# W_out's weight sums by VectorE from blocks on chip, and another order of loads and evictions around the last head pair

## The chip, the cores and the metric

The kernel runs on one core of one Trainium2 chip. The metric is the device time of one execution in microseconds (us). The times of before are three runs: 539.84, 540.49 and 540.99 us, median 540.49. The trace comes from one further, profiled execution.

## The reference, cut to what matters

One layer of a bidirectional trunk on a sequence of 512 positions and a model width of 1024, in float32. The change touches the output projection `mix @ w_out` of the attention half, and what stands around it.

```python
h = rms_norm(x, attn_norm_g)
xr, gate, q, k, v = split(h @ w_in)
y_rnn  = (rg_lru_fwd(conv(xr)) + rg_lru_bwd(conv(xr))) * gelu(gate)
y_attn = dilated_attention(q, k, v, rel_bias)      # 8 heads of 64
mix = concat(rms_norm(y_rnn, norm_rnn_g), rms_norm(y_attn, norm_attn_g))   # 512 + 512 columns
x = x + mix @ w_out                                # w_out: 1024 x 1024
h = rms_norm(x, mlp_norm_g)
x = x + square(relu(h @ w_up)) @ w_down
return rms_norm(x, final_norm_g)
```

## The kernel before, in words

**Products of three.** TensorE (PE) multiplies in a reduced float32. Each operand is split into a rounded part "hi" and a remainder "lo", and a product is three matmuls: hi·hi, hi·lo and lo·hi (`mm3`, L323 to L325). "A product" below means these three matmuls on a 128x128 by 128x512 tile. A weight tile of 128x1024 (512 KB) is split by `conv_hi` (L252, a copy by ScalarE, ACT) and `conv_lo` (L279, a subtraction by VectorE, DVE). Weights come through a stream of three buffers named `wraw`. `emit_dma` (L235) loads the next of the list `plain` each time `conv_lo` has freed a buffer.

**Attention.** Heads are handled in pairs 0 to 3, a pair in four quarters u = 0 to 3. For a pair and a quarter, PE computes the scores (`att_s`, L829, tile `ps` in two PSUM banks "gs"). DVE adds the bias and takes the extreme value (`att_e`, L846, one instruction per head, reading a bias tile `tw`), POOL (GpSimd) zeroes the edge of the tile (L845), and ACT takes the exponential (L847). One step of the outer loop later PE transposes the quarter (`att_t`, L867, tile `pt`) and ACT copies it out (L869). `att_av` (L969, tile `pav`) multiplies by the values. DVE then multiplies by the reciprocal sums `zrow`, giving `yp` (L975). The path to `zrow` is: reciprocal and spread by DVE (`att_z`, L891 and L893), a transpose by PE (`att_zt`, L897, tile `prow`), a copy by ACT (L898), and four transfers from SP's queue (`att_zd`, L905). `att_q` squares `yp` on ACT (L623), `att_y` adds the square to a running sum on DVE (L629), and `att_a` scales `yp` on ACT into `at` (L986). When all four pairs are in, PE turns the sum (L441, tile `pcs`), DVE reduces it (L446, L425) and POOL raises it to the power -1/2 (L428, `rcol`). Every eviction of the attention half of W_out needs this `rcol`.

Bias tiles: for each head and each of two variants, `load_tw` (L494 to L499) issues one transfer of 128x384 and two of 128x160 from a table in HBM into one of four `tw` buffers of 128x1024.

**Fillers.** Between these steps the loop `for i in range(5): for u in range(4)` puts independent products from a list (`fill`): first the projections of q and k, then 32 products of the recurrent half of W_out (`wo_thunks`), called b0 to b31 here. b0 to b15 make the left column half for the four row tiles tt, b16 to b31 the right half. A table `FILL` says how many fillers stand at the four places of a quarter; without an entry it is one each. After the fourth product of a row tile, DVE adds the PSUM tile to the residual: `x <- pwo` (L1022). In before this addition follows directly behind its last product on DVE's queue. When b0 comes up, `load_x` is called; it starts the loads of the residual x (eight tiles of 256 KB, L1064) and of W_out's attention half, spread over the following quarters by the list `more`.

**W_out's attention half by seven products.** The 2x2 block product is made with seven block products instead of eight (Winograd's form). The weights are four blocks named 11, 12, 21, 22 (512 KB each). Needed are 11, 21, 22 and the sums s1 = 11+12, s2 = 11+12+22, s3 = 12+22, s4 = 11+12+22+21, up to signs. The order of use is `OSEQ` = 11, s2, s3, s4, 21, s1, 22, four products each (`wo_m`, evicted by `wo_x`, L1205). In before the sums are made by the transfers. For each sum a plain load puts the first block into a part of the tile `ws` (L1067, SP's queue), and every further block is a transfer with `accum_op=add` from POOL's queue (L1070). Blocks 11, 21 and 22 come once more through the `wraw` stream. The row sums on the activation side (`o_sum`, `o_hi`, `o_lo`, `o_hi2`, `o_lo2`) are made by DVE and ACT from `at`. For 21 and s1 the remainder is made by `remake` (L262, L264): two negative copies by ACT, and two accumulating transfers from POOL's queue.

**Behind it** stands the up projection. Its first tiles n0, n1, n2 come through `wraw`, and its first sums t1, t2, t3 are loaded into `tw` buffers by `load_t` (L1180) and completed by accumulating transfers from POOL's queue (L1182).

**What sets the order.** The instructions of PE, ACT, DVE and POOL stay in the order in which the program issues them; each engine works through its list in order. The order of SP's transfers is set by the compiler's scheduler. A transfer waits for its buffer, and in SP's list each waits for the one eight places ahead of it. `BES` holds what stands beside each of the 28 products of the seven.

## Time and profile of before

The profiled execution took 539.57 us on the device; its span from the first to the last instruction was 537.8 us.

| | before |
|---|---|
| runs (us) | 539.84, 540.49, 540.99 |
| profiled execution | 539.57 us, span 537.8 us |
| granted TensorE clock, mean | 0.997 |
| PE busy | 525.1 us, 98% |
| DVE busy | 429.9 us, 80% |
| ACT busy | 358.4 us, 67% |
| POOL busy | 77.0 us, 14% |
| moved by DMA | 112.29 MB |

In a timeline a line has the start, the duration, the engine, the line of the code, the operation, what it writes and reads, and a count. In brackets stands the engine's idle time before it and what ended it. PE is a pipeline: the next matmul starts 0.23 us after the one before although each is listed as 0.39 us, so lost time is read from the starts. In the view of waits each line has who waited for whom, the sum in us, how often, and the longest.

### The profile page before, as it was taken

The numbers are of one execution on the slowest core, as the hardware profiler recorded it, in microseconds if no ns is written. First come the engines' busy times: TensorE is split into PE (matmuls) and PEld (weight loads), VectorE is DVE, ScalarE is ACT, GpSimd is POOL, SyncE is SP. The second block draws the span as 40 slices with busy tenths as digits, with TensorE's granted clock in tenths as the row PEclk, the third lists the DMA queues.
The fourth block names the chain that finished last, engine by engine and source line by source line (L and its number), as shares of the span: only waits on it lengthen the run. The fifth ranks groups of instructions, "written<-read, shape, count | busy, mean of one in ns | idle before, by whom it ended". The sixth has DMA issues, their size and how long they took to land.

```text
span 537.8 us, 8418 instructions
## 1 busy us (share of the span) xinstructions
PE 525.1 (98%) x3035; PEld 451.7 (84%) x3035; DVE 429.9 (80%) x636; ACT 358.4 (67%) x578; POOL 77.0 (14%) x128
## 2 busy tenths in 40 slices
PE   9999999999989889999999999999999999999995
PEld 7757888887877668889999888888999999888884
DVE  6998888996843688889769987879756978886985
ACT  7578946888845556586566855565656686755665
POOL 0282000000102241001030223001001120131000
PEclk9999999999999999999999999999999999999998
DMA  7745386687699969966686799994987497799804
GB/s 280 234 135 139 88 234 179 159 255 192 147 304 299 296 112 235 345 209 168 185 163 165 201 247 275 278 369 116 289 236 202 126 207 188 179 290 261 206 1 157
DMA packets 44298, 112.29 MB, mean 209 GB/s; under 512 B 5332, under 2 KB 15700, under 8 KB 44256
## 3 DMA queue, kind: packets, MB, share of 16 engines
q1 hardware_dynamic: 35536, 81.71, 46.1%
q0 software_dynamic: 8544, 29.81, 29.6%
q8 instruction: 24, 0.39, 0.3%
q10 hardware_dynamic: 176, 0.23, 0.1%
q14 instruction: 18, 0.15, 0.1%
HBM read 100.16 MB, written 4.23 MB: 194 GB/s over the span
## 4 chain that ended last, share of the span: by engine, by line
PE 86%; DMA 7%; DVE 4%; issue 1%; ACT 0%; SPq 0%; POOL 0%; DVEq 0%; ACTq 0%; POOLq 0%
PE pu L324 10%; PE pu L325 10%; PE pu L323 10%; PE pd L324 9%; PE pd L323 9%; PE pd L325 9%; PE pqk L323 3%; PE pqk L325 3%; PE pqk L324 3%; DMA tw<-in_w_up_dram 2%; PE ps L829 2%; DMA zrow<-z 2%; PE pv L323 2%; PE pt L867 1%; PE pg L543 1%; PE pwo L323 1%
## 5 line engine op out<-in xcount | busy, mean ns | idle before, releaser
L279 DVE TENSOR_TENSOR wlo<-wraw,whi 128x1024 fp32r<-128x1024 f32 x72 | 87.8, 1220 | 21.1 <-ACT whi L252 20.7
L252 ACT ACTIVATE whi<-wraw 128x1024 fp32r<-128x1024 f32 x69 | 72.9, 1058 | 39.3 <-PE pd L325 18.4
L324 PE MATMUL pd<-wlo,ah 128*128 128x512 f32 (+1 forms) x195 | 75.2, 386 | 0.0
L323 PE MATMUL pd<-whi,ah 128*128 128x512 f32 (+1 forms) x195 | 75.2, 386 | 0.0
L325 PE MATMUL pd<-whi,al 128*128 128x512 f32 (+1 forms) x195 | 75.2, 386 | 0.0
L252 ACT ACTIVATE whi<-tw 128x1024 fp32r<-128x1024 f32 x36 | 38.0, 1059 | 38.1 <-PE pu L324 8.1
L325 PE MATMUL pu<-hh,wlo 128*128 128x256 f32 x224 | 63.4, 283 | 0.0
L324 PE MATMUL pu<-hl,whi 128*128 128x256 f32 x224 | 63.4, 283 | 0.0
L323 PE MATMUL pu<-hh,whi 128*128 128x256 f32 x224 | 63.4, 283 | 0.0
L323 PE MATMUL pu<-h2h,whi 128*128 128x256 f32 (+1 forms) x200 | 60.1, 300 | 0.0
L324 PE MATMUL pu<-h2l,whi 128*128 128x256 f32 (+1 forms) x200 | 60.0, 300 | 0.0
L325 PE MATMUL pu<-h2h,wlo 128*128 128x256 f32 (+1 forms) x200 | 60.0, 300 | 0.0
L279 DVE TENSOR_TENSOR wlo<-tw,whi 128x1024 fp32r<-128x1024 f32 x36 | 44.0, 1222 | 18.4 <-ACT whi L252 18.3
L323 PEld LDWEIGHTS pu<-hh,whi 128*128 128x128 f32 x224 | 43.0, 192 | 0.0
L324 PEld LDWEIGHTS pu<-hl,whi 128*128 128x128 f32 x224 | 43.0, 192 | 0.0
L325 PEld LDWEIGHTS pu<-hh,wlo 128*128 128x128 f32 x224 | 43.0, 192 | 0.0
L325 PEld LDWEIGHTS pd<-whi,al 128*128 128x128 f32 x195 | 36.6, 188 | 7.4
L323 PEld LDWEIGHTS pd<-whi,ah 128*128 128x128 f32 x195 | 36.6, 188 | 7.4
L252 ACT ACTIVATE whi<-ts 128x1024 fp32r<-128x1024 f32 x24 | 25.5, 1061 | 26.0 <-PE pd L325 18.4
L324 PEld LDWEIGHTS pd<-wlo,ah 128*128 128x128 f32 x195 | 36.6, 188 | 7.2
L323 PEld LDWEIGHTS pu<-h2h,whi 128*128 128x128 f32 x200 | 38.3, 191 | 1.3
L324 PEld LDWEIGHTS pu<-h2l,whi 128*128 128x128 f32 x200 | 38.3, 191 | 1.3
(281 smaller groups left out, 1262.3 us busy)
## 6 DMA issues: line engine op xcount, KB each, us to landing
wraw<-in_w_up_dram SPq DMA_DIRECT2D x25, 512.0 KB, 3.8
ts<-in_w_dn_dram POOLq DMA_DIRECT2D x24, 512.0 KB, 13.3
wraw<-in_w_dn_dram SPq DMA_DIRECT2D x24, 512.0 KB, 9.6
tw<-in_w_up_dram SPq DMA_DIRECT2D x15, 512.0 KB, 9.8
tw<-in_w_up_dram POOLq DMA_DIRECT2D x15, 512.0 KB, 8.4
wraw<-in_w_in_dram SPq DMA_DIRECT2D x13, 512.0 KB, 4.1
ts<-in_w_dn_dram SPq DMA_DIRECT2D x8, 512.0 KB, 8.9
tw<-in_w_dn_dram SPq DMA_DIRECT2D x8, 512.0 KB, 8.5
```

The lines of the kernel that those rows point to most:

```text
L252: act(hi, raws[i], AF.Copy)
L279: nc.vector.tensor_tensor(lo, r, f(splits[i][0]), op=OP.subtract)
L323: nc.tensor.matmul(o, lhsT=a[0], rhs=b[0], start=bool(first), stop=False, skip_group_check=on)
L324: nc.tensor.matmul(o, lhsT=a[0], rhs=b[1], start=False, stop=False, skip_group_check=on)
L325: nc.tensor.matmul(o, lhsT=a[1], rhs=b[0], start=False, stop=bool(last), skip_group_check=on)
L543: nc.tensor.matmul(pg[2 * d + j][halves[b ^ d]], lhsT=gwr[t][halves[b], c], rhs=xc[t][halves[b]], start=True, stop=True)
L829: nc.tensor.matmul(psq[p][e][:, :NK], lhsT=sp[p, 0, n, e][:, c0:c0 + P], rhs=k, start=i == 0, stop=i == 1)
L867: nc.tensor.transpose(pt[:, i * P:(i + 1) * P], en[h][qt][:, k:k + P], ident)
```

## The change

Five things are changed:

1. `load_x`: only the blocks 12, 22 and 21 are loaded (SP's queue), and 11 comes through `wraw` as before. DVE makes the sums: `sum1` s1 = 12+11, `sum2` s2 = s1+22 (into a `tw` buffer), `sum3` s3 = 12+22 in place, and s4 = s2+21 (another `tw` buffer). All seven accumulating transfers of L1070 go, and so do the second loads of 21 and 22 through `wraw`.
2. `load_tw`: the two transfers of 128x160 become one with a pattern of 128x2x160.
3. `FILL`: three fillers instead of four in the first three quarters of step 3. The three products stand later instead, between the last `att_av` and the turn `pcs`, and behind that.
4. The addition `x <- pwo` of a row tile is put off to a later product (`end`), and the last one to behind the four products of block 11.
5. Around the last pair: `att_a` ahead of `att_q`; the row sums s1 and s2 of the second half, and the splits of the weights (`conv_hi`, `conv_lo`), stand at other products.

```diff
-    plain = deque(i for i, c in enumerate(chunks) if c is not None and not (isinstance(c, tuple) and c[1][0] in "st"))
+    plain = deque(i for i, c in enumerate(chunks) if c is not None and not (isinstance(c, tuple) and (c[1][0] in "st" or c[0] == "o" and c[1] != "11")))
...
-        for c, k in ((0, TH - WN - v), (WN + TH + P, P - 1 + v)):
-            nc.sync.dma_start(t[:, c:c + WN], bass.AP(tensor=nbd.tensor, offset=b + S + k, ap=[[1, P], [1, WN]]))
+        k = TH - WN - v
+        nc.sync.dma_start(bass.AP(tensor=t.tensor, offset=t.offset, ap=[t.ap[0], [WN + TH + P, 2], [1, WN]]),
+                          bass.AP(tensor=nbd.tensor, offset=b + S + k, ap=[[1, P], [P - 1 + v - k, 2], [1, WN]]))
...
+            if p == 3:
+                att_a(p)
             if p != 2:
                 att_q(p)
+            if p < 2:
                 att_a(p)
...
+        def end(n, tt):
+            stt(x1[tt, n], pw[n, tt], rc[0][:, tt:tt + 1], x1[tt, n], op0=OP.mult, op1=OP.add)
...
-                if b in (1, 17, 21, 25):
-                    conv_hi(C_WO + {1: 3, 17: 4, 21: 5, 25: 6}[b])
-                if b in (3, 19, 23, 26):
-                    conv_lo(C_WO + {3: 3, 19: 4, 23: 5, 26: 6}[b])
-                if k == 3:
-                    stt(x1[tt, n], o, rc[0][:, tt:tt + 1], x1[tt, n], op0=OP.mult, op1=OP.add)
+                if b in (1, 15, 18, 28):
+                    conv_hi(C_WO + {1: 3, 15: 4, 18: 5, 28: 6}[b])
+                if b in (3, 17, 20):
+                    conv_lo(C_WO + {3: 3, 17: 4, 20: 5}[b])
+                if n == 0 and tt and k == 3:
+                    end(0, tt - 1)
+                if n and (tt, k) == (0, 1):
+                    end(0, 3)
+                if n and k == 3 and tt < 3:
+                    end(1, tt)
             return run
+        st["wo"] = lambda: end(1, 3)
...
-        def w_add(n, b):
-            return lambda: nc.gpsimd.dma_start(ts[n], oblock(b), accum_op=OP.add)
+        def sum1():
+            tt(s1, b12, raws[C_WA], op=OP.add)
+
+        def sum2():
+            t = work.tile([P, 1024], FT, name="tw", tag="tw", bufs=4)
+            tt(t, s1, b22, op=OP.add)
+            chunk("s2", t)
+            t4 = work.tile([P, 1024], FT, name="tw", tag="tw", bufs=4)
+            chunk("s4", t4)
+            more[1].append(lambda: tt(t4, t, b21, op=OP.add))
+
+        def sum3():
+            tt(b12, b12, b22, op=OP.add)
...
+        w_in(b12, "12")()
         x_in(0, 0)()
-        x_in(1, 0)()
-        more.append([x_in(2, 0), x_in(3, 0), w_in("s2", "11")])
-        more.append([w_add("s2", "12"), w_in("s3", "12")])
-        more.append([w_add("s2", "22"), w_in("s4", "11")])
-        more.append([w_add("s3", "22"), w_add("s4", "12"), w_in("s1", "11")])
-        more.append([w_add("s4", "22"), w_add("s1", "12")])
-        more.append([w_add("s4", "21"), x_in(0, 1), x_in(1, 1)])
+        more.append([x_in(1, 0), w_in(b22, "22")])
+        more.append([x_in(2, 0), x_in(3, 0)])
+        more.append([sum1, w_in(b21, "21")])
+        more.append([sum2, x_in(0, 1)])
+        more.append([sum3, x_in(1, 1)])
         more.append([x_in(2, 1), x_in(3, 1)])
...
-    FILL = {(4, 0): (0, 1, 0, 0), (4, 1): (0, 1, 0, 1), (4, 2): (0, 1, 0, 0), (4, 3): (0, 1, 0, 0)}
+    FILL = {(3, 0): (1, 1, 1, 0), (3, 1): (1, 1, 1, 0), (3, 2): (1, 1, 1, 0), (4, 0): (0, 1, 0, 0), (4, 1): (0, 1, 0, 1), (4, 2): (0, 1, 0, 0), (4, 3): (0, 1, 0, 0)}
...
     fill(1)
     att_av(3, range(4))
-    att_y(3)
-    o_lo2(0)
-    fill(3)
-    rc[1] = rstd_cols(row_sums(turned(ssy[1], "gs")), S)
-    remake(C_WA + OSEQ.index("21"))
+    fill(1)
     o_sum("s1", 1)
     o_sum("s2", 1)
     o_hi("s2", 1)
+    fill(1)
+    att_y(3)
+    o_lo("s2", 1)
+    fill(3)
+    rc[1] = rstd_cols(row_sums(turned(ssy[1], "gs")), S)
+    fill(1)
+    conv_lo(C_WA + 2)
+    remake(C_WA + OSEQ.index("21"))
     fill(len(fillers))
...
-    BES["11"].update({1: lambda: (o_lo("s2", 1), o_hi2(1))})
-    BES["11"].update({2: lambda: o_lo("s1", 0)})
-    BES["21"].update({2: lambda: o_lo("22", 0)})
-    BES["s2"].update({1: lambda: o_lo2(1), 2: lambda: o_hi("s1", 1)})
-    BES["s3"].update({1: lambda: (o_lo("s1", 1), o_sum("22", 1)), 2: lambda: o_hi("22", 1)})
-    BES["s4"].update({1: lambda: o_lo("22", 1)})
-    BES["11"].setdefault(1, lambda: None)
-    also = BES["11"][1]
-    BES["11"][1] = lambda: (also(), remake(C_WA + OSEQ.index("s1")))
+    BES["11"].update({1: lambda: (o_hi2(1), remake(C_WA + OSEQ.index("s1"))), 3: lambda: st["wo"]()})
+    BES["s2"].update({1: lambda: conv_lo(C_WA + 3), 2: lambda: o_hi("s1", 1), 3: lambda: (conv_lo(C_WA + 4), o_lo2(0))})
+    BES["s3"].update({1: lambda: o_lo2(1)})
+    BES["s4"].update({1: lambda: (o_lo("s1", 0), o_sum("22", 1)), 2: lambda: o_hi("22", 1)})
+    BES["21"].update({1: lambda: o_lo("s1", 1), 3: lambda: (conv_lo(C_WA + 7), o_lo("22", 0), o_lo("22", 1))})
```

On the engines' lists this reads as follows. DVE gets four additions of 128x1024 and the same number of everything else. POOL's list loses the seven transfers. SP's list loses two loads of W_out, one of the first `ws` loads, and one transfer in each pair of bias transfers. PE and ACT have the same instructions in another order.

More of the change, by code (lines that the diff above doesn't have):

```diff
@@ L266, in emit_plain @@
     def emit_plain(i):
-        if chunks[i][1][0] != "s":
+        if chunks[i] == ("o", "11"):
             emit_dma()
@@ L282, in conv_lo @@
             if isinstance(c, tuple) and c[0] == "o":
-                if c[1][0] != "s":
+                if c[1] == "11":
                     emit_dma()
@@ L1057, in load_x, with chunk @@
         ws = big.tile([P, 4, 1024], FT, name="ws", tag="bigB")
-        ts = {n: ws[:, i, :] for i, n in enumerate(("s2", "s3", "s4", "s1"))}
-        for n, t in ts.items():
+        b12, b22, b21, s1 = [ws[:, i, :] for i in range(4)]
+        tt = nc.vector.tensor_tensor
+        def chunk(n, t):
             raws[C_WA + OSEQ.index(n)] = t
@@ L1064, in x_in, with w_in @@
             return lambda: nc.sync.dma_start(x1[g, n], xn[2 * g + n])
-        def w_in(n, b):
-            return lambda: nc.sync.dma_start(ts[n], oblock(b))
-        def w_add(n, b):
-            return lambda: nc.gpsimd.dma_start(ts[n], oblock(b), accum_op=OP.add)
-        x_in(0, 0)()
-        x_in(1, 0)()
-        more.append([x_in(2, 0), x_in(3, 0), w_in("s2", "11")])
-        more.append([w_add("s2", "12"), w_in("s3", "12")])
-        more.append([w_add("s2", "22"), w_in("s4", "11")])
-        more.append([w_add("s3", "22"), w_add("s4", "12"), w_in("s1", "11")])
-        more.append([w_add("s4", "22"), w_add("s1", "12")])
-        more.append([w_add("s4", "21"), x_in(0, 1), x_in(1, 1)])
+        def w_in(t, b):
+            return lambda: nc.sync.dma_start(t, oblock(b))
+        def sum1():
[9 more added lines that the diff above has]
+            tt(b12, b12, b22, op=OP.add)
+        for n, t in (("s3", b12), ("22", b22), ("21", b21), ("s1", s1)):
+            chunk(n, t)
+        w_in(b12, "12")()
+        x_in(0, 0)()
+        more.append([x_in(1, 0), w_in(b22, "22")])
[3 more added lines that the diff above has]
+        more.append([sum3, x_in(1, 1)])
         more.append([x_in(2, 1), x_in(3, 1)])
```

## The prediction

> **What bounds the kernel now.** I read the page first, then PE's waits, then the timelines around them.
>
> ```profile
> span 537.8 us, 8418 instructions
> PE 525.1 (98%) x3035; PEld 451.7 (84%) x3035; DVE 429.9 (80%) x636; ACT 358.4 (67%) x578; POOL 77.0 (14%) x128
> ```
>
> PE is the bound, and 12.7 us of the span are not its own. The view of its waits, whole trace, says which of these can be had:
>
> ```profile
> PE pcs L441 <- DVE ysq L629: 2.0, 1, 2.0
> PE pt L867 <- POOL e L845: 2.0, 1, 2.0
> PE prow L897 <- DVE z L893: 1.4, 1, 1.4
> ```
>
> These are three single waits; the view's two others are shorter and stand at the start, and the rest is the first load and the tail. All three lie around the last head pair. PE's timeline there:
>
> ```profile
> 152.16 0.39 PE L325 MATMUL pwo<-whi,yl 128*128 128x512 f32 x1
> 153.98 0.30 PE L897 MATMUL prow<-ident,z 128*128 128x128 f32 x1 [1.44 <-DVE z L893]
> ...
> 154.82 0.35 PE L829 MATMUL ps<-kk,qh 128*128 128x416 f32 x1
> ...
> 159.21 0.35 PE L829 MATMUL ps<-kk,qh 128*128 128x416 f32 x1
> ...
> 177.93 0.40 PE L325 MATMUL pwo<-whi,yl 128*128 128x512 f32 x1
> 180.30 1.09 PE L867 MATMUL pt<-ident,e 128*128 128x128 f32 x8 [1.97 <-POOL e L845]
> ...
> 184.29 3.02 PE L969 MATMUL pav<-ett,vs 128*64 128x416 f32 x24
> ...
> 189.20 0.40 PE L325 MATMUL pwo<-whi,yl 128*128 128x512 f32 x1
> 191.62 0.66 PE L441 MATMUL pcs<-ident,ysq 128*128 128x128 f32 x4 [2.02 <-DVE ysq L629]
> ...
> 192.81 0.40 PE L323 MATMUL pwo<-whi,oh 128*128 128x512 f32 x1
> ...
> 195.33 0.39 PE L325 MATMUL pwo<-whi,ol 128*128 128x512 f32 x1
> ...
> 198.97 0.50 PE L323 MATMUL pwo<-whi,oh 128*128 128x512 f32 x1
> ```
>
> Undisturbed, twelve starts take 195.33 - 192.81 = 2.52 us, 0.229 a step and 0.69 a product. Start to start, less one step, the three gaps lose 1.59, 2.14 and 2.19 us. From 192.81 to 198.97 stand 24 steps, 5.50 us undisturbed and 6.16 in the trace: 0.66 lost at the heads of products s2 and s3. Together 6.58 us.
>
> Why each gap is there, by the timelines of DVE, POOL and SP's queue and by the chain of waits:
>
> ```profile
> 151.69 0.75 DVE L1022 SCALAR_TENSOR_TENSOR x<-pwo,rcol,x 128x512 f32<-128x512 f32 x1 [3.01 <-DMA x<-in_xn_dram]
> ...
> 153.61 0.23 DVE L893 COPY z<-rz 128x128 f32<-128x128 f32 x1
> ...
> 163.29 0.59 DVE L846 CUSTOM_DVE_ANT_0 e<-ps,tw 128x416 f32<-128x416 f32 x1 [2.91 <-DMA tw<-nbd]
> ```
> ```profile
> 178.31 1.76 POOL L1070 DMA_DIRECT2D ws<-in_w_out_dram  x2 [11.85 <-DMA ws<-in_w_out_dram]
> 179.40 0.96 POOL L845 MEMSET e<- 128x96 f32 x2
> ```
> ```profile
> 176.25 2.65 SPq L905 DMA_DIRECT2D zrow<-z  x4
> ```
> ```profile
> 178.36 10.94 DMA zrow<-z
> ```
>
> First gap: the first residual addition stands ahead of the scores' eviction and of z in DVE's list, and waits for its x. Second: the memsets for the last quarter stand in POOL's list behind two accumulating transfers, which wait 11.85 us for earlier ones. Third: the last zrow transfer is 10.94 us under way, so yp, its square and the turn come late. The last two are transfers in each other's way; the window view shows how full the DMA engines are:
>
> ```profile
> 150.00:158.00 8.00, 6.57 (x37) 5.43 (x36) 3.88 (x12) 4.38 (x12) 1.30 (x3) 1.00 1.04 395
> 158.00:162.00 4.00, 4.00 (x24) 3.48 (x24) 1.35 (x3) 1.81 (x5) 0.00 (x0) 1.00 1.03 232
> ```
>
> The last two columns are the DMA share and GB/s: full in both, but at 232 instead of 395 GB/s once accumulations and bias tiles run.
>
> **The change part by part.**
>
> *Traffic.* By the code, 14 transfers of 512 KB bring W_out's attention half (three through wraw, four plain, seven accumulating); four remain. 10 x 0.524 = 5.2 MB go, which at 232 to 395 GB/s is 13 to 23 us of the engines' time.
>
> *Second gap.* POOL's list then has only memsets here, none behind a transfer. The full 2.14 us are taken as gone; were a memset still late, 0 to 2.14 would stay.
>
> *First gap.* The addition now follows z in DVE's list. At three products a quarter PE still makes b6 to b8 before prow, reaching it at 152.39; z then has only the two evictions ahead. They need the second head's bias tile:
>
> ```profile
> 144.34 0.91 SPq L498 DMA_DIRECT2D tw<-nbd  x2
> 145.34 2.60 SPq L1064 DMA_DIRECT2D x<-in_xn_dram  x4
> ```
> ```profile
> tw<-nbd SPq DMA_DIRECT2D x14, 80.0 KB, 4.7
> ws<-in_w_out_dram SPq DMA_DIRECT2D x4, 512.0 KB, 6.7
> ```
> ```profile
> DMA to landing us min/median/max: 4.3/7.4/13.4
> ```
>
> (The issues by line have the median time to landing last; the third view is of the ws tile, its eleven transfers of both queues.) Issued by 145.25 with 4.7 us to landing it is there at 150.0; one transfer fewer only helps. Eviction 0.59 (the row at 163.29), reciprocal about 0.2 and z 0.23: z ends near 151.3, a microsecond ahead of PE. The 1.59 us go.
>
> *DVE's four additions.* No row has this instruction; the nearest is the subtraction of the same shape from two on-chip tiles:
>
> ```profile
> 197.05 1.21 DVE L279 TENSOR_TENSOR wlo<-ws,whi 128x1024 fp32r<-128x1024 f32 x1
> ```
>
> 1.21 each, 4.8 us in all. A quarter of step 3 then asks DVE for two evictions (1.2), one residual addition (0.75, row 151.69) and one sum (1.21): 3.2 us. PE's quarter shrinks from 159.21 - 154.82 = 4.39 to 3.70, one product less. So 0.5 us are free in each, and the sums hide behind PE. Uncovered they would cost 4.8; below nothing isn't possible, since DVE makes nothing less.
>
> *The bias tiles of the last two quarters.* They are queued behind 12, two x, 22, kk, n1 and two x: 2.9 MB, from 150.0 on at 395 GB/s until 157.3. Two tiles of 352 KB follow, 0.72 MB at 395 to 232 GB/s: the second lands between 159.1 and 160.4, its eviction (0.59) ends between 159.7 and 161.0. PE, without the first gap and three products shorter, comes to the fourth quarter's scores at 159.21 + 4.37 - 1.59 - 2.07 = 159.9 and needs the second bank 0.4 later. So 0 to 0.7 us are lost; I take 0.4. The bound above is the landing of before (row 163.29, eviction ended 163.88): 3.5.
>
> *Third gap.* The last pav starts at 184.29 less both gaps and three products, 178.5, and ends near 181.4 (3.02, less the pipeline's overlap). zrow is issued 3.7 us earlier than at 176.25, the last of the four near 174.8, so it has 6.6 us. Ahead of it in SP's list stand three loads of 512 KB (n2, and two for t1 and t2), issued once DVE frees a wraw buffer near 166: 1.6 MB, 4 us at 395 GB/s, gone by 171. Taken: in time. With the 10.94 us of before it would land at 185.7 and cost 3.3. Five products, 3.45 us, now stand between this pav and pcs, instead of three. The chain on DVE and ACT:
>
> ```profile
> 189.48 0.69 DVE L975 TENSOR_TENSOR yp<-pav,zrow 128x512 f32<-128x512 f32 x1 [1.95 <-DMA zrow<-z]
> 190.87 0.69 DVE L629 TENSOR_TENSOR ysq<-ysq 128x512 f32<-128x512 f32 x1 [0.69 <-ACT ysq L623]
> ...
> 193.53 0.42 DVE L946 TENSOR_TENSOR osum<-at 128x256 f32<-128x256 f32 x1
> ```
>
> Some 0.25 until yp, 0.69, on DVE then a residual addition 0.75, two row sums 0.42 each, and the sum of squares 0.69: 3.2 us. (On ACT, at and the square end earlier.) The margin is 0.2 us; I leave 0.1 standing. Without the two products moved here 1.2 would be lost.
>
> *The head of s2 and s3.* From pcs PE has its own 0.44 and six products (4.12): s2 at 4.56. DVE has the sum of squares until 0.2 before pcs, then a split of 0.42 and two residual additions of 0.75, until 1.7 after it, then
>
> ```profile
> 192.74 0.68 DVE L446 TENSOR_REDUCE cs<-pcs 128x4 f32<-128x512 f32 x1
> 193.45 0.17 DVE L425 TENSOR_SCALAR rv<-cs 128x4 f32<-128x4 f32 x1
> ```
> ```profile
> 193.71 1.14 POOL L428 TENSOR_TENSOR rcol<-rv,mhalf 128x4 f32<-128x4 f32 x1 [6.28 <-DVE rv L425]
> ```
>
> 0.68, 0.17, rcol 1.14, the first eviction 0.75, and 0.3 of hand-overs (an estimate: 0.1 each, as from 193.62 to 193.71): 4.7. 0.1 lost at s2. At s3 a conversion of 1.21 stands between two evictions as before: 0.25, and 0.1 at s4. I put 0.45 against the 0.66.
>
> A conversion now runs on DVE beside rcol. The start of the kernel shows the same pair:
>
> ```profile
> 22.48 1.34 POOL L428 TENSOR_TENSOR rcol<-rv,mhalf 128x4 f32<-128x4 f32 x1 [18.73 <-DVE rv L425]
> ...
> 22.96 1.23 DVE L279 TENSOR_TENSOR wlo<-wraw,whi 128x1024 fp32r<-128x1024 f32 x1
> ```
>
> rcol took 1.34 and ended (23.82) before the conversion did (24.19): 0 to 0.2 more than 1.14, 0.1 taken. [...]
>
> *Moved loads behind it.* Two tw buffers now hold s2 and s4, so the load for the second group's t1 waits until s4 is converted, near 193, instead of issuing at 167. It stalls nothing: PE waits for no load anywhere after 199, and SP's next load waits for a wraw buffer until about then in before too. Zero; with that cover gone, its landing time.
>
> *Sum.* Lost now 6.58; left 0.4 + 0.1 + 0.45 + 0.1 = 1.05. Gain 5.5. The profiled execution, 539.57 on the device around its span of 537.8, would be 534.0; the median of runs is 540.49, 0.9 above it, so 534.9. Bounds: all of it gone, 540.5 - 6.6 = 533.9, less 0.6 of spread between runs; the bias tiles or zrow as late as before, 538.2.
>
> **The rivals.**
>
> 1. *Bias tiles as late as before.* 3.1 us more than taken: 538.0. For it: they share a queue with as many bytes as before. Against: the accumulation at 155 is gone.
> 2. *zrow as slow as before.* It lands at 185.7: 3.3 us, 538.2. For it: three loads stand right ahead of it, as four did. Against: they are issued 6 us earlier, and no accumulation runs beside; up to 6.6 us under way costs nothing.
> 3. *Slower: DVE's list waits for block 12.* sum1 stands ahead of the evictions of the second quarter. Issued near 145.3, with the plain 6.7 us, block 12 is there at 152.0, when DVE comes to it. Each microsecond beyond 153 holds up scores and transposes one for one. With the 13.4 us of the longest ws transfer it lands at 158.7: 5.7 us, all of the gain. The bias tiles of the third quarter, eight places behind in SP's list, are then issued so late that about 1 us more is lost: 541.6. It decides from 158.5 on. Against: that longest transfer ran beside accumulations.
> 4. *rcol waits until the conversion beside it has ended.* For it: both read on-chip tiles, and the conversion starts first. Against: the rows at 22.48 and 22.96. Price 1.1 us (1.21 less the 0.1 taken): 536.0.
> 5. *The change does not do what it says.* The three waits are replaced by others of the same size, since DVE and SP serve the same deadlines: 540.5.
>
> **How the numbers follow.** Forecast 0.68, its own range 533.3 to 536.2; rival 1 0.09, rival 2 0.07, rival 3 0.08, rival 4 0.03, rival 5 0.05. About 0.2% (1.1 us) is what a measurement tells from no change. Faster: forecast and rivals 1, 2, 4, 0.87; same: rival 5, 0.05; slower: rival 3, 0.08. The range goes from 533.3 to 538.2, with rivals 3 and 5 outside.
>
> **What would show it.** PE's waits must lose pt behind POOL and prow behind z, and pcs behind ysq must fall below 0.3. DMA must move about 107 MB instead of 112.29. Bias tiles: the wait of the eviction e for tw in the last two quarters, below 1.5 us without a wait of ps. The sums: DVE must wait for no ws transfer. rcol under 1.4 us. Wrong would be a new wait of PE's ps or pt for DVE above 1 us.

## The result, and the profile after

The changed kernel takes 534.99 us, the median of four runs (533.74, 534.94, 535.03 and 536.40), beside 540.24 us for the kernel before on the same chip. The ratio is 0.9902 with a 95% interval of 0.9875 to 0.9929, so about 5.3 us are gained. Measured twice more, on other occasions, the medians are 535.11 and 534.97 us, and the ratios 0.9898 [0.9880, 0.9916] and 0.9901 [0.9884, 0.9918].

The profiled execution of the changed kernel is its longest run, 536.40 us. That matters below: some of what its trace shows is larger there than in two further traces of the same program. First its page:

```profile
span 534.6 us, 8387 instructions
...
DMA packets 42602, 107.05 MB, mean 200 GB/s; under 512 B 4916, under 2 KB 15284, under 8 KB 42560
```

5.24 MB less are moved than before, ten blocks of 0.524 MB as counted. PE's waits in the same trace:

```profile
PE ps L830 <- DVE mn L847: 1.3, 1, 1.3
...
PE pwo L323 <- DVE x L1231: 0.2, 1, 0.2
```

The three waits of before (pcs, pt, prow) are gone from the list. Two new ones of this stretch stand there: the scores `ps`, and the head of product s2. The line numbers have moved: L830 was L829, L847 was L846, the evictions `wo_x` are L1231, the residual additions L1014. PE's timeline at the places of the three old gaps and of the two new ones:

```profile
144.09 0.40 PE L323 MATMUL pwo<-whi,yh 128*128 128x512 f32 x1
...
153.33 0.39 PE L325 MATMUL pwo<-whi,yl 128*128 128x512 f32 x1
153.56 0.27 PE L898 MATMUL prow<-ident,z 128*128 128x128 f32 x1
...
161.36 0.35 PE L830 MATMUL ps<-kk,ql 128*128 128x416 f32 x1
163.06 0.45 PE L830 MATMUL ps<-kk,qh 128*128 128x416 f32 x1 [1.35 <-DVE mn L847]
...
178.62 0.39 PE L325 MATMUL pwo<-whi,yl 128*128 128x512 f32 x1
178.85 1.04 PE L868 MATMUL pt<-ident,e 128*128 128x128 f32 x8
...
187.48 0.39 PE L325 MATMUL pwo<-whi,yl 128*128 128x512 f32 x1
187.71 0.60 PE L441 MATMUL pcs<-ident,ysq 128*128 128x128 f32 x4
...
192.03 0.39 PE L325 MATMUL pwo<-whi,ol 128*128 128x512 f32 x1
192.66 0.50 PE L323 MATMUL pwo<-whi,oh 128*128 128x512 f32 x1 [0.25 <-DVE x L1231]
...
198.45 0.39 PE L323 MATMUL pwo<-whi,oh 128*128 128x512 f32 x1
```

prow, the last pt and pcs each start one step (0.23 us) behind the matmul ahead of them: all three gaps are zero. At 163.06 the second bank of the last quarter's scores is 1.70 us behind the matmul before it, one step of which is 0.19: 1.51 us lost. s2 (192.66) loses 0.40. The first row is b0, the last the head of product s4; these two instants bound the stretch that the change touches. DVE in that stretch:

```profile
154.70 1.22 DVE L1084 TENSOR_TENSOR ws<-ws,wraw 128x1024 f32<-128x1024 f32 x1
...
157.51 1.22 DVE L1088 TENSOR_TENSOR tw<-ws 128x1024 f32<-128x1024 f32 x1
160.41 0.59 DVE L847 CUSTOM_DVE_ANT_0 e<-ps,tw 128x416 f32<-128x416 f32 x1 [1.68 <-DMA tw<-nbd]
...
162.41 0.59 DVE L847 CUSTOM_DVE_ANT_0 e<-ps,tw 128x416 f32<-128x416 f32 x1 [1.40 <-DMA tw<-nbd]
...
189.59 0.17 DVE L425 TENSOR_SCALAR rv<-cs 128x4 f32<-128x4 f32 x1
189.67 1.22 DVE L279 TENSOR_TENSOR wlo<-ws,whi 128x1024 fp32r<-128x1024 f32 x1
191.78 0.17 DVE L1265 TENSOR_SCALAR nrc<-rcol 128x4 f32<-128x4 f32 x1 [0.90 <-POOL rcol L428]
```

The first two sums (154.70, 157.51) take 1.22 us and start without an idle time: no wait for a block. The other two (162.92, 169.16) do the same. The evictions of the last quarter wait 1.68 and 1.40 us for their bias tiles. POOL's power, beside the conversion of 189.67:

```profile
189.84 1.91 POOL L428 TENSOR_TENSOR rcol<-rv,mhalf 128x4 f32<-128x4 f32 x1 [25.90 <-DVE rv L425]
```

It takes 1.91 us instead of 1.14 in before. The transfers of zrow, by the view of that tile's issues from 150 to 184 (the last line of the answer):

```profile
DMA to landing us min/median/max: 2.1/2.1/5.8
```

In before the same view says 4.9/10.8/12.1. The view holds two head pairs; the four transfers of the last pair land 2.1 us after their issue, and the 5.8 belongs to the pair before it. The next table gives starts of PE read from the timelines; "a0" and "a1" are the two further traces of the changed kernel.

| | before | after | a0 | a1 |
|---|---|---|---|---|
| profiled execution, us | 539.57 | 536.40 | 535.11 | 534.11 |
| start of b0 | 142.91 | 144.09 | 143.82 | 143.02 |
| start of s4 | 201.82 | 198.45 | 197.15 | 196.15 |
| b0 to s4 | 58.91 | 54.36 | 53.33 | 53.13 |
| s4 to the last matmul | 329.80 | 329.85 | 329.84 | 329.86 |

Behind s4 nothing changes. In the stretch from b0 to s4 the change gains 4.55, 5.58 and 5.78 us. Ahead of b0 the trace of after is 1.18 us later than before's. 0.54 of this are there at the very first scores (96.40 beside 95.86); a0 and a1 have them at 96.26 and 95.40, so this part varies from one execution to the next. 0.63 are lost between 110 and 117, which experiments 1 and 2 look into.

### The profile page after: what moved, and what is told of

The parts are those of the page before. It is cut to its first block, busy times and chain, and to the rows that moved or that the text cites. A ratio compares the mean times of both kernels' runs of the same rounds, so it can differ in the third digit from the quotient of the medians.

```text
span 534.6 us, 8387 instructions
## 1 busy us (share of the span) xinstructions
PE 525.5 (98%) x3035; PEld 451.3 (84%) x3035; DVE 434.6 (81%) x640; ACT 359.1 (67%) x578; POOL 72.3 (14%) x121
## 4 chain that ended last, share of the span: by engine, by line
PE 85%; issue 8%; DVE 3%; DMA 1%; POOL 1%; SPq 0%; ACT 0%; DVEq 0%; POOLq 0%; ACTq 0%
PE pu L324 10%; PE pu L323 10%; PE pu L325 10%; PE pd L323 9%; PE pd L324 9%; PE pd L325 9%; PE pqk L323 3%; PE pqk L325 3%; PE pqk L324 3%; PE ps L830 2%; PE pv L323 2%; PE pg L544 1%; PE pv L324 1%; PE pp L323 1%; PE pp L325 1%
## 5 line engine op out<-in xcount | busy, mean ns | idle before, releaser
L279 DVE TENSOR_TENSOR wlo<-wraw,whi 128x1024 fp32r<-128x1024 f32 x71 | 86.7, 1221 | 23.2 <-ACT whi L252 22.8
L252 ACT ACTIVATE whi<-wraw 128x1024 fp32r<-128x1024 f32 x67 | 70.8, 1059 | 37.0 <-PE pd L325 19.3
L252 ACT ACTIVATE whi<-tw 128x1024 fp32r<-128x1024 f32 x38 | 40.2, 1060 | 39.4 <-DMA tw<-in_w_up_dram 12.0
L279 DVE TENSOR_TENSOR wlo<-tw,whi 128x1024 fp32r<-128x1024 f32 x38 | 46.5, 1222 | 19.1 <-ACT whi L252 19.1
L325 PEld LDWEIGHTS pu<-h2h,wlo 128*128 128x128 f32 x200 | 38.3, 191 | 1.3
```

The lines of the kernel that those rows point to most:

```text
L252: act(hi, raws[i], AF.Copy)
L279: nc.vector.tensor_tensor(lo, r, f(splits[i][0]), op=OP.subtract)
L325: nc.tensor.matmul(o, lhsT=a[1], rhs=b[0], start=False, stop=bool(last), skip_group_check=on)
```

## The experiments

Twelve runs were made, of ten kernels. They ask what the small new losses are and whether they belong to the program (1 to 4), what each part of the change is worth alone (5, 6), what slack is left (7, 8), and whether a better version follows (9).

**1. The changed kernel again** (two runs of the same program, a0_after and a1_after).

> The changed kernel once more, to see which of its small losses come back. If they belong to the program: PE waits about 1.5 us for the second bank of the last quarter's scores (161.4 to 163.1), some 0.6 us are lost between 110 and 117 behind a late ql, rcol takes about 1.9 us and s2 starts 0.4 us late; the time is 534 to 536. If they are chance of one execution: at least two of the four are gone or below half.

> The changed kernel once more, beside e9_again on one chip: 534.5 to 535.5, with the same late s2 (0.40 us) and a wait for the second bank of the last quarter's scores between 0.4 and 1.5 us.

535.11 us (534.71 to 535.92) and 534.97 us (534.11 to 535.79). PE in a0 at 110, at the prow behind it and at the second bank, and then PE in a1 at 110:

```profile
110.54 0.35 PE L830 MATMUL ps<-kk,qh 128*128 128x416 f32 x1
110.73 0.35 PE L830 MATMUL ps<-kk,ql 128*128 128x416 f32 x1
...
114.17 0.30 PE L898 MATMUL prow<-ident,z 128*128 128x128 f32 x1 [0.16 <-DVE z L894]
...
161.00 0.35 PE L830 MATMUL ps<-kk,ql 128*128 128x416 f32 x1
161.77 0.46 PE L830 MATMUL ps<-kk,qh 128*128 128x416 f32 x1 [0.42 <-DVE mn L847]
```
```profile
109.68 0.35 PE L830 MATMUL ps<-kk,qh 128*128 128x416 f32 x1
110.01 0.46 PE L830 MATMUL ps<-kk,ql 128*128 128x416 f32 x1
```

0.77 - 0.19 = 0.58 us are lost at the second bank, and 0.39 in a1, against 1.51 in the first trace. The loss between 110 and 117 comes back in both, not always in the same place. a0 loses nothing at 110, but its prow at 114.17 is 0.31 late: the eviction ahead of z begins only after 1.31 us of idle time on DVE. a1 loses 0.14 at 110 (109.68 to 110.01, less 0.19), as after does, and more behind it. From the first scores to b0 PE takes 47.05 us in before, 47.69 in after, 47.57 in a0 and 47.62 in a1. rcol (1.91) and s2 (0.40 and 0.41) come out the same each time. So three of the four losses belong to the program, and the second bank's, below half in both, varies from one execution to the next.

**2. Bias tiles by three transfers again.**

```diff
-        k = TH - WN - v
-        nc.sync.dma_start(bass.AP(tensor=t.tensor, offset=t.offset, ap=[t.ap[0], [WN + TH + P, 2], [1, WN]]),
-                          bass.AP(tensor=nbd.tensor, offset=b + S + k, ap=[[1, P], [P - 1 + v - k, 2], [1, WN]]))
+        for c, k in ((0, TH - WN - v), (WN + TH + P, P - 1 + v)):
+            nc.sync.dma_start(t[:, c:c + WN], bass.AP(tensor=nbd.tensor, offset=b + S + k, ap=[[1, P], [1, WN]]))
```

> Each bias tile again by three transfers (one of 128x384, two of 128x160) instead of two. Theory (the merged transfer stands ahead of the second ql in SP's list and makes it land late): that ql lands 3 to 4 us after its issue instead of 5.9, and PE's delay of 0.6 us between 110 and 117 is gone. Rival (the ql is late for other reasons, such as the traffic of the moment): the delay stays. In the last two quarters 1 transfer more for each tile either costs nothing (the wait for the second bank stays 1.5 us) or makes it 0.3 to 1 us longer.

535.66 us, ratio 0.9904 [0.9883, 0.9924]. The view of the two ql transfers of pair 1 in SP's queue, first of a0 and then of this kernel:

```profile
DMA to landing us min/median/max: 3.2/4.4/5.7
```
```profile
DMA to landing us min/median/max: 3.2/3.2/3.2
```

The second ql stands behind the merged transfer in SP's list. In all seven traces with the merged transfer there it lands 5.7 to 6.1 us after its issue. In the seven traces with two separate ones, the kernel before among them, the view rests on one landing, that of the first ql (3.1 to 3.5 us); it has none for the second. The single packets in the traces settle it: the last packet of the second ql ends 2.4 to 2.6 us after the issue with separate transfers, and 4.8 to 5.2 us after it with the merged one. The late landing costs PE at the scores only where the issue is late as well: issued at 104.53 (a0) it is in time, at 105.15 (experiment 3's trace) PE waits 0.4 us for it and 0.55 are lost, and here an issue at 105.13 costs nothing.

The late ql is not the whole loss between 110 and 117. From the first scores to b0 this kernel takes 47.22 us, and the other six with separate transfers there take 47.04 to 47.37 and, in one case, 47.60: `best` (experiment 9), whose prow is 0.35 late behind a bias tile. Of the seven with the merged transfer six take 47.55 to 48.11, and experiment 4's takes 47.11. Nor is it shown that the merging does it. Merged, both strips of 128x160 stand ahead of the second ql; separate, one of them stands behind it. No run puts two separate strips ahead.

The other side: with one transfer more for each tile the second bank loses 1.05 us here, more than in a0 and a1 and less than in the first trace of after. So the theory holds for the ql, and the time shows no gain.

**3. Two residual loads behind the last bias tiles.**

```diff
-        more.append([x_in(2, 0), x_in(3, 0)])
-        more.append([sum1, w_in(b21, "21")])
-        more.append([sum2, x_in(0, 1)])
+        more.append([])
+        more.append([sum1, w_in(b21, "21"), x_in(2, 0)])
+        more.append([sum2, x_in(3, 0), x_in(0, 1)])
```

> The loads of x(2,0) and x(3,0) are put behind the last pair's second two bias tiles in SP's list. Theory (the bias tiles are late because SP issues them only once transfers eight places ahead have landed, and two x loads of 256 KB stand right ahead): the tiles are issued about 2 us earlier, PE's wait for the second bank of the last quarter falls from 1.5 us to below 0.3, and the time is 1 to 1.5 us shorter. Rival (the tiles share the DMA engines with whatever else is under way): the issues come earlier but the landing hardly does, and the wait stays above 1 us.

534.84 us, ratio 0.9888 [0.9869, 0.9908]: not to be told from the changed kernel. SP now issues the strips of the two tiles at 152.78 and 154.12 instead of 153.89 and 155.55 in a0. DVE's two evictions:

```profile
158.58 0.59 DVE L847 CUSTOM_DVE_ANT_0 e<-ps,tw 128x416 f32<-128x416 f32 x1 [0.34 <-PE ps L830]
...
161.22 0.59 DVE L847 CUSTOM_DVE_ANT_0 e<-ps,tw 128x416 f32<-128x416 f32 x1 [2.04 <-DMA tw<-nbd]
```

The first tile is now there before PE's scores are. The second, issued 1.4 us earlier, lands at 161.1, where it landed in a0 (161.0). Of the two readings each is right for one tile: the first was late by its issue, and the second was not. That what moves beside it holds it fits, but no run shows this alone. PE's loss at the second bank is 0.25 us, 0.14 to 0.33 less than in a1 and a0; a gain of 1 to 1.5 us is not there.

**4. No conversion beside rcol.**

```diff
     fill(1)
-    conv_lo(C_WA + 2)
     remake(C_WA + OSEQ.index("21"))
...
-    BES["11"].update({1: lambda: (o_hi2(1), ...
+    BES["11"].update({1: lambda: (conv_lo(C_WA + 2), o_hi2(1), ...
```

> The conversion of s3 is put behind the first eviction of product 11, so that no VectorE instruction with two on-chip inputs runs beside rcol. Theory (POOL's rcol is held while such an instruction runs): rcol takes 1.0 to 1.2 us instead of 1.91, nrc follows at once, and s2 starts without its wait of 0.4 us; a few tenths may come back at s2's second half, where the conversion now stands ahead of an eviction. Rival (rcol's length is something else, such as its place behind a long pause of POOL): it stays near 1.9 us.

534.61 us, ratio 0.9892 [0.9868, 0.9917]. POOL's timeline, and PE's at the head of s2:

```profile
188.14 1.01 POOL L428 TENSOR_TENSOR rcol<-rv,mhalf 128x4 f32<-128x4 f32 x1 [25.88 <-DVE rv L425]
```
```profile
190.32 0.39 PE L325 MATMUL pwo<-whi,ol 128*128 128x512 f32 x1
190.55 0.39 PE L323 MATMUL pwo<-whi,oh 128*128 128x512 f32 x1
```

rcol is back at 1.01 us, and s2 starts without a loss (0.23, one step). At s2's second half 0.08 and at s3's second half 0.22 us are lost instead (in a0 0 and 0.08), because the conversion now stands between the evictions of product 11 and delays those behind it. From the head of 11 to the head of s4 PE takes 8.76 us, against 8.93 in a0: 0.17 gained, as the trace shows it; too little for the medians.

**5. The kernel before, with the residual additions of the first column half put off, and nothing else.**

```diff
-                if k == 3:
-                    stt(x1[tt, n], o, rc[0][:, tt:tt + 1], x1[tt, n], op0=OP.mult, op1=OP.add)
+                if n == 0 and tt and k == 3:
+                    end(0, tt - 1)
+                if n and (tt, k) == (0, 1):
+                    end(0, 3)
+                if n and k == 3:
+                    end(1, tt)
```

> The kernel before, with one part of the change alone: each residual addition of the first half of the columns is put off by one product, so that the first no longer stands ahead of z in VectorE's list. Theory (the second gap is set by transfers that end at their own time, full DMA engines from 150 on, and the bias tiles are late too): the 1.59 us in front of prow go, but PE waits as much longer for ps or pt, and the time falls by 0 to 0.5 us, not 1.6. Rival (the transfers move forward with PE, or the gaps are independent): the time falls by 1.4 to 1.7 us.

540.69 us beside 540.86, ratio 1.0004 [0.9987, 1.0021]: nothing. PE's waits:

```profile
PE pt L867 <- POOL e L845: 2.4, 1, 2.4
PE pcs L441 <- DVE ysq L629: 1.9, 1, 1.9
PE ps L829 <- DVE mn L846: 1.8, 1, 1.8
```

The wait for prow is gone, and in its place PE waits 1.8 us for the scores (DVE sits idle 3.7 us for a bias tile) and 0.4 more for pt. The 1.59 us of the first gap were not to be had alone: the transfers came at their own time, and PE, earlier by that much, waited longer for them.

**6. The kernel before, with the sums on VectorE, and nothing else.** `load_x` is that of the change, with the three edits that go with it; the other parts of the change are left out.

```diff
-    plain = deque(i for i, c in enumerate(chunks) if c is not None and not (isinstance(c, tuple) and c[1][0] in "st"))
+    plain = deque(i for i, c in enumerate(chunks) if c is not None and not (isinstance(c, tuple) and (c[1][0] in "st" or c[0] == "o" and c[1] != "11")))
...
-        if chunks[i][1][0] != "s":
+        if chunks[i] == ("o", "11"):
...
-                if c[1][0] != "s":
+                if c[1] == "11":
```

> The kernel before, with the weight sums on VectorE and the loads that go with them, and nothing else: bias tiles by three transfers, the old places of the residual additions, four products in each quarter of step 3, the old order behind the last pav. Theory (the traffic makes most of the loss): POOL's memsets are no longer late and the 2.14 us before pt go, zrow lands within 6 us and the wait of pcs falls from 2.0 to below 1.3 us, the first gap stays at 0.8 to 1.6 us; together 3 to 4.3 us faster than before. Rival (the order of the lists makes most of it): less than 2 us faster, with new waits of PE for VectorE where the sums stand in its list.

538.42 us, ratio 0.9959 [0.9944, 0.9975]: about 2.2 us faster (0.9959 of 540.86), and not the 3 to 4.3 expected. The profiled execution is the longest of its ten runs, 540.62 us. PE:

```profile
154.03 0.39 PE L325 MATMUL pwo<-whi,yl 128*128 128x512 f32 x1
157.52 0.30 PE L897 MATMUL prow<-ident,z 128*128 128x128 f32 x1 [3.10 <-DVE z L893]
```

No wait for pt is left, the last pair's zrow lands 2.1 us after its issue, and pcs, 2.19 us late in before, is 0.17 late, with the old order behind the last pav. So the second and the third gap both went with this part alone, the accumulating transfers and the loads that they needed. The first gap has doubled, to 3.26 us: in the new `load_x` block 12 stands ahead of x(0,0), and the addition, still ahead of the evictions and of z, waits 4.68 us for its x. The window view of that stretch (its last three columns are the granted clock, the DMA share and GB/s) shows a second price:

```profile
154.00:157.50 3.50, 0.42 (x2) 0.01 (x1) 2.23 (x8) 0.98 (x3) 0.00 (x0) 1.00 1.05 406
157.50:159.00 1.50, 1.48 (x6) 1.30 (x7) 1.50 (x2) 0.66 (x3) 0.00 (x0) 0.73 1.03 391
159.00:161.00 2.00, 2.00 (x10) 1.84 (x9) 1.37 (x5) 0.04 (x1) 0.00 (x0) 0.50 1.20 327
161.00:163.00 2.00, 2.00 (x11) 1.74 (x10) 0.00 (x0) 1.67 (x5) 0.00 (x0) 0.85 0.63 188
```

After the 3.1 us without work the granted clock falls to 0.50. From prow to the second matmul behind pt PE takes 4.31 us (157.52 to 161.83); in experiment 5, at full clock, the same stretch takes 2.67 (152.62 to 155.29). So 1.6 us more are lost.

**7. Three products back in the quarters of step 3.**

```diff
-    FILL = {(3, 0): (1, 1, 1, 0), (3, 1): (1, 1, 1, 0), (3, 2): (1, 1, 1, 0), (4, 0): (0, 1, 0, 0), (4, 1): (0, 1, 0, 1), (4, 2): (0, 1, 0, 0), (4, 3): (0, 1, 0, 0)}
+    FILL = {(4, 0): (0, 1, 0, 0), (4, 1): (0, 1, 0, 1), (4, 2): (0, 1, 0, 0), (4, 3): (0, 1, 0, 0)}
```

> The changed kernel with four products instead of three in each of the first three quarters of step 3, so that three products fewer stand behind the last pair: one fewer between the last pav and pcs, two fewer between pcs and s2. Theory (those products cover the chain on VectorE and POOL): pcs waits 0.2 to 0.5 us, s2 starts 1.5 to 2.2 us late instead of 0.4, and the wait for the second bank, 0.6 us or more, goes since PE comes there later; 0.7 to 2 us slower than the changed kernel. Rival (the products are as good in the quarters): no difference above 0.5 us.

537.54 us, ratio 0.9945 [0.9924, 0.9967]: 2.6 us slower than a1 beside it. PE's waits:

```profile
PE pwo L323 <- DVE x L1231: 1.1, 1, 1.1
PE pcs L441 <- DVE ysq L630: 0.8, 1, 0.8
...
PE ps L830 <- DMA ql<-ql: 0.5, 1, 0.5
PE pt L868 <- ACT e L848: 0.5, 1, 0.5
```

With one product fewer ahead of it pcs loses 0.96 us, with two fewer ahead of it s2 loses 1.23 instead of 0.41, and one pt waits 0.46 for the exponential. The wait for the second bank is gone, as expected. From b0 to s4 PE takes 55.39 us, 2.26 more than in a1: 0.96 + 0.82 + 0.46 - 0.39, and 0.4 in small pieces. That is above the 2 us expected at most, since pcs lost twice what was expected and the wait of pt wasn't foreseen. (The late ql of this trace stands ahead of b0 and is not in the sum.) The moved products do cover the chain, and none is to spare.

**8. The first two sums made twice.**

```diff
-            tt(s1, b12, raws[C_WA], op=OP.add)
+            for _ in range(2):
+                tt(s1, b12, raws[C_WA], op=OP.add)
...
-            tt(t, s1, b22, op=OP.add)
+            for _ in range(2):
+                tt(t, s1, b22, op=OP.add)
```

> The changed kernel with the first two of the four sums made twice, 1.21 us more of VectorE's time in each of two quarters. Theory (about half a microsecond is free in the first quarter, where the sum stands ahead of both evictions, and over a microsecond in the second, where VectorE waits for a bias tile anyway): 0.4 to 1 us are lost at the transposes of the quarter behind the first sum, nothing at the second, and as PE comes later to the last quarter its wait for the second bank shrinks: 0 to 0.7 us slower. Rival 1 (there is no free time): 2 us or more slower. Rival 2 (VectorE isn't near the path): no loss in front of pt or ps beyond the wait for the bias tiles.

535.09 us, ratio 0.9900 [0.9877, 0.9923]: no slower. DVE:

```profile
154.27 2.48 DVE L1085 TENSOR_TENSOR ws<-ws,wraw 128x1024 f32<-128x1024 f32 x2
...
158.34 2.48 DVE L1090 TENSOR_TENSOR tw<-ws 128x1024 f32<-128x1024 f32 x2
160.73 0.58 DVE L847 CUSTOM_DVE_ANT_0 e<-ps,tw 128x416 f32<-128x416 f32 x1
```

Behind the first pair the four score matmuls of the next quarter start over 0.81 us (157.30 to 158.11) instead of 0.57, so 0.24 are lost there, at ps and not at pt as expected. Behind the second pair the eviction starts without a wait for its tile: the time was idle anyway, and the second bank loses 0.16. From b0 to s4 PE takes 53.40 us, beside 53.33 in a0 and 53.13 in a1. Rival 2 is the nearer one: even twice the work in these two quarters lies beside PE.

**9. Versions put together.** `best` has the edits of experiments 3 and 4, and of 2 for pairs 0 to 2 alone. `e7_stt` adds one: the residual addition of row tile 2 goes from ahead of cs to behind rv, beside rcol. `e9_again` is `e7_stt` beside a1.

```diff
-                if n and k == 3 and tt < 3:
+                if n and k == 3 and tt < 2:
                     end(1, tt)
...
          st["wo"] = lambda: end(1, 3)
+        st["wo2"] = lambda: end(1, 2)
...
     rc[1] = rstd_cols(row_sums(turned(ssy[1], "gs")), S)
+    st["wo2"]()
     fill(1)
```

> The changed kernel with three edits: the conversion of s3 behind the first eviction of product 11, the bias tiles of pairs 0 to 2 again by three transfers, x(2,0) and x(3,0) behind the last bias tiles. Theory: the second ql of pair 1 lands 3 to 4 us after its issue, the wait for the second bank stays under 0.4 us, rcol takes 1.0 to 1.2 us; 0.4 to 1.2 us shorter than the changed kernel, 533.9 to 534.7. Rival (these losses are already covered or come back at the next wait): within 0.3 us of the changed kernel's 535.1.

> As the combined version, and one residual addition more (one input in PSUM, one on chip, 0.75 us) is moved from ahead of cs to behind rv, so that it runs on VectorE beside rcol. Theory (only an instruction with two on-chip inputs holds rcol back): rcol takes 1.0 to 1.2 us beside it, cs starts about 0.6 us earlier, s2 and s3 start without any loss, 0.1 to 0.4 us less than the combined version. Rival (any VectorE instruction beside it holds it): rcol ends 0.85 to 0.9 us after the addition has ended, 1.4 us or more in all, and nothing is gained.

> The version of e7_stt once more, beside a1_after on one chip. Theory (its gains are those of its trace: s2 0.3 us earlier, no late ql, a shorter wait for the bias tiles, less 0.15 at s3): 0.4 to 1.2 us below a1_after. Rival (534.02 was a favourable set of runs): within 0.3 us of it.

best 534.67 us, ratio 0.9882 [0.9861, 0.9903]; e7_stt 534.02 us, 0.9873 [0.9850, 0.9896]; e9_again 534.03 us (533.43 to 534.38), 0.9883 [0.9865, 0.9901], 0.94 us below a1's 534.97 on the same chip. The intervals of the ratios overlap with the changed kernel's, so 0.9 us is the best estimate and not more. The profiled executions of e9_again and a1 differ by 0.06 us (534.05 and 534.11), and in them b0 to s4 takes 52.76 and 53.13 us: 0.37 of the 0.94 is seen in a trace (0.14 behind the head of 11, 0.22 at the second bank). Where the rest comes from no trace shows. Nor does a trace show what the moved addition adds to best: from b0 to s4 best takes 52.44 us and e7_stt 53.11, the other way round than their medians. In best the second bank loses 0.01 us and the last packet of the second ql ends 2.4 us after its issue, as expected.

DVE and POOL around rcol in e7_stt:

```profile
187.57 0.74 DVE L1018 SCALAR_TENSOR_TENSOR x<-pwo,rcol,x 128x512 f32<-128x512 f32 x1
```
```profile
187.74 1.01 POOL L428 TENSOR_TENSOR rcol<-rv,mhalf 128x4 f32<-128x4 f32 x1 [25.36 <-DVE rv L425]
```

Beside an addition with one input in PSUM and one on chip rcol keeps its 1.01 us. What this frees does not reach PE: s3's second half still loses 0.22 us, because the conversion between the evictions is untouched. Without any loss, as expected, it did not go.

## Why the prediction was right, and where it was not

Forecast were 534.9 us, in a range of 533.3 to 538.2; 534.99, 535.11 and 534.97 were measured. The sum by its terms:

| us left over | predicted | after | a0 | a1 |
|---|---|---|---|---|
| first gap, prow | 0 | 0 | 0 | 0 |
| second gap, pt | 0 | 0 | 0 | 0 |
| bias tiles, second bank | 0.4 (0 to 0.7) | 1.51 | 0.58 | 0.39 |
| third gap, pcs | 0.1 | 0 | 0 | 0 |
| heads of s2 to s4, with rcol | 0.55 | 0.68 | 0.69 | 0.68 |
| gain from b0 to s4 | 5.5 | 4.55 | 5.58 | 5.78 |

(The fifth row is the time from the head of 11 to the head of s4, less 36 steps of 0.229 us.)

That the medians meet the forecast to 0.2 us is partly luck. In a0 and a1 the stretch gained up to 0.3 more than forecast, and the 0.5 to 0.6 us lost ahead of b0 had no term in the sum. The medians of before on the four occasions lie between 540.03 and 540.94.

- *First gap:* right, and so was its reason, but only together with the rest. Experiments 5 and 6 show what the sum took for granted. The addition put off is worth nothing alone (540.69 beside 540.86), the sums on VectorE alone 2.2 us, the whole change 5.1 to 5.8. The parts don't add up: closing the first gap alone only moved the wait to ps and pt, whose ends were set by transfers that came at their own time, and the sums alone made the first gap longer. No run has these two parts together without the rest, and of the rest the three moved products are worth 2.6 us (experiment 7). The prediction took all three gaps out at once, which is right for the change as a whole; as a sum of separate gains it would have been wrong.
- *Second gap:* right. Without accumulating transfers in POOL's list there is no wait for the memset, in after and in experiment 6 alike (0 us lost at pt, where before lost 2.14).
- *Third gap:* right by two covers, both shown. The last pair's zrow lands 2.1 us after its issue, where 6.6 were allowed; in a0 the sum of squares ends at 185.99 and PE reaches pcs at 186.40, a margin of 0.4 where 0.2 was worked out. Experiment 7 takes products away and pays 0.96 at pcs and 0.82 more at s2; the prediction gave 1.2 for two products at pcs.
- *The four additions:* right that they hide behind PE. The free time was underrated: 0.5 us per quarter were worked out, and 1.2 more in each of two quarters cost 0.24 (experiment 8). The quarter's other term, the wait for a bias tile, holds DVE idle in any case.
- *Bias tiles:* the mechanism was right, and for a0 and a1 the size too. The first trace, 1.51 us, is outside "0 to 0.7" and inside the bound of 3.5. It also shows the sign that the prediction called wrong, a wait of ps for DVE above 1 us (1.35 there, 0.42 in a0, 0.2 in a1). The step that was mis-sized is the spread: SP issues these tiles at different times (155.93 in that trace, 155.18 in a0, for the last tile), and the bounds came from one execution.
- *"One transfer fewer only helps":* wrong for pair 1. The ql behind the merged transfer in SP's list is under way some 2.5 us longer, and the scores at 110 start 0.09 to 0.63 us late in five of the seven traces that have it. With a late prow behind them in most, which best has too, 0.5 to 1.1 us are lost ahead of b0 in six of the seven. The prediction asked what the merged transfer means for its own tile, and not for the transfer that stands behind it.
- *rcol:* the step misread its row. It took 0.1 us more for rcol beside the conversion, arguing from rows 22.48 and 22.96 that rcol doesn't wait. But there rcol had begun before that conversion (22.48 and 22.96), so the row could not show whether it would wait. In the changed kernel the conversion begins first (189.67, rcol 189.84), rcol takes 0.9 us longer, above the 1.4 that were named as the sign, and 0.40 us are lost at s2, where 0.1, and 0.1 more for rcol, were taken.
- *Rival 4*, for which the prediction had no row, therefore came: rcol takes 1.91 us beside the conversion and 1.01 without it (experiment 4). Its price was too high: 1.1 us were worked out for it, but taking the conversion away gains 0.32 at s2 and gives 0.15 of it back at once.
- *Rivals 1, 2, 3 and 5* did not come: the tiles cost 0.4 to 1.5 and not 3.5, zrow was in time, DVE waited for no block, and in a0 and a1 no wait near the old size took the place of the old ones. (The price of rival 2 was too low by its own chain: a zrow at 185.7 instead of 181.65 (181.4 and 0.25), less the margin of 0.2, is 3.9 us and not 3.3.)
- *Moved loads:* zero, as forecast. From s4 to the last matmul all kernels take 329.80 to 329.89 us.

## What to carry to other kernels

When several stalls in a row end on transfers, closing one of them can move the wait to the next (experiment 5: the 1.59 us at prow went, and 1.8 at ps and 0.4 more at pt came): cost the parts of a change together, and test each alone before calling it the cause. A merged or longer transfer is to be weighed for what stands behind it in its queue (here a ql, 4.8 to 5.2 us under way instead of 2.4 to 2.6). And a row shows that two instructions don't hold each other back only if the one that would wait began second (here rcol began at 22.48 and the conversion at 22.96).

## What the runs showed of the hardware that was not expected

*POOL held by VectorE.* rcol's length by what runs on VectorE beside it: 1.91 us in all seven traces with the conversion beside it, which reads two on-chip tiles; 1.01 with nothing beside it; 1.01 beside an addition that reads one on-chip tile and one in PSUM. With the conversion it ends 0.86 us after that has ended (189.67 + 1.22 = 190.89, and 189.84 + 1.91 = 191.75). The rows of before fit: the row sum that began first, at 193.53, ends at 193.95, and rcol at 194.85, 0.90 later. So does the rcol of the prediction's pair, which took 1.34 us. Ahead of the conversion stands a copy that began before it:

```profile
22.23 0.69 DVE L250 CAST whi<-wraw 128x1024 fp32r<-128x1024 f32 x1
```

The copy ends at 22.92, and rcol ends 0.90 later, at 23.82. In after the same three rows give 0.90 again (the copy ends at 23.45, rcol at 24.35). So the row that was read as no hold fits a hold by the copy. This copy reads one on-chip tile only; which instructions of one on-chip input hold rcol, the runs don't show.

*The clock behind a long gap.* PE without work for 3.10 us (experiment 6) was followed by a granted clock of 0.73, 0.50 and 0.85 over the next 1.5, 2 and 2 us, and 1.6 us more were lost than the gap itself. Behind the gaps of 2.0 us in before, and of 2.35 in experiment 5, the granted clock stayed at 1.00. So in this trace a gap of 3.1 us cost half as much again as it shows. It is one trace; how often this comes, no run shows.

*A transfer behind a merged one.* With two strips of 128x160 as one transfer ahead of it, the last packet of the second ql ended 4.8 to 5.2 us after its issue; with one strip ahead and the other behind it, 2.4 to 2.6 us after, in seven traces each. By which resource it is held, and whether two separate strips ahead of it would do the same, the runs don't show.

*What an accumulating transfer takes.* The DMA queues of before from 164 to 170, where q0 is POOL's queue and holds accumulating transfers alone (packets, MB, share of the 16 engines' time):

```profile
q1 hardware_dynamic: 671, 1.30, 58.1%
q0 software_dynamic: 154, 0.58, 48.2%
```

At full share the plain transfers would move 1.30 / (6 x 0.581) = 0.373 MB a us, and the accumulating ones 0.58 / (6 x 0.482) = 0.200: an estimate from this window. By this estimate a byte of the seven accumulating transfers that the change removes took nearly twice the engines' time of a plain one, and the ten removed transfers took 3.67 / 0.200 + 1.57 / 0.373 = 22.6 us of that time, the upper end of the prediction's 13 to 23.
